# A maximum over the last axis: four blocks with their own partition pitch in place of one pitch of 512 KB

## The chip, the cores and the metric

The kernel runs on one core of a Trainium2 chip. The metric is the device time of one execution in microseconds (us); lower is better. Medians of several runs are quoted. The "span" of a profile (164.7 us for the kernel before) is about 1.8 us shorter than the device time of that same execution (166.5 us).

## The reference

```python
x = np.random.randn(32, 512, 1024).astype(np.float32)
def reference(x):
    return np.max(x, axis=-1).astype(np.float32)
```

These are 16,384 rows of 1,024 floats (4 KB each, 67.1 MB in all), and one maximum per row. Spread over 128 partitions, each partition has 128 rows.

## The kernel before

One queue (SyncE's) loads groups of rows into a ring buffer of 46 rows per partition. VectorE takes the maximum of each group as soon as it has landed. The number of rows of each group is in `ROWS`; the groups become smaller so that little work is left when the last one lands.

```python
ROWS = [10, 13, 12, 10, 9, 8, 7, 7, 6, 5, 5, 4, 4, 3, 3, 3, 3, 2, 2, 2, 2, 2, 1, 1, 1, 1, 1]
RING = 46
...
xr = xf.rearrange("(p i) d -> p i d", p=P)      # partition p holds rows 128p .. 128p+127
...
for g in ROWS:
    if at + g > RING:
        at = 0
    xc = ring[:, at:at + g, :]
    nc.sync.dma_start(out=xc, in_=xr[:, b:b + g, :])
    nc.vector.reduce_max(out=res[:, b:b + g], in_=xc, axis=X)
    at += g
    b += g
    if not stored and b >= I - 16:
        stored = b
        nc.scalar.dma_start(out=out_r[:, :b], in_=res[:, :b])
# the last row in two halves
for h in range(2):
    xh = ring[:, at, h * H:(h + 1) * H]
    nc.sync.dma_start(out=xh, in_=xr[:, b, h * H:(h + 1) * H])
    nc.vector.reduce_max(out=part[:, h:h + 1], in_=xh, axis=X)
nc.vector.tensor_tensor(...max of the two halves...)
nc.scalar.dma_start(out=out_r[:, stored:], in_=res[:, stored:])
```

A load of g rows reads 4g KB in one piece for each partition. One such piece is a packet in the profile, and a load has landed when all 128 of its packets are in. The pieces of neighbouring partitions start 128 x 4 KB = 512 KB apart in memory. This distance is the pitch.

Of the kernel before, what the change touches and what calls it, by code (L numbers as in the profile page):

```python
# [1 line left out]

# [4 lines left out]


F32 = mybir.dt.float32


ROWS = [10, 13, 12, 10, 9, 8, 7, 7, 6, 5, 5, 4, 4, 3, 3, 3, 3, 2, 2, 2, 2, 2, 1, 1, 1, 1, 1]
RING = 46


@with_exitstack
def kernel(
    ctx: ExitStack,
    tc: tile.TileContext,
    x: bass.AP,  # L20
    out: bass.AP,
):
    nc = tc.nc
    P = 128
    X = mybir.AxisListType.X

    xf = x.flatten_outer_dims()
    N, D = xf.shape
    H = D // 2
    I = N // P  # L30

    xr = xf.rearrange("(p i) d -> p i d", p=P)
    of = out.flatten_outer_dims()
    out_r = bass.AP(tensor=of.tensor, offset=of.offset, ap=[[I, P], [1, I]])

    once = ctx.enter_context(tc.tile_pool(name="once", bufs=1))
    ring = once.tile([P, RING, D], F32)
    res = once.tile([P, I], F32)
    part = once.tile([P, 2], F32)

    b = at = 0
    stored = 0
    for g in ROWS:
        if at + g > RING:
            at = 0
        xc = ring[:, at:at + g, :]
        nc.sync.dma_start(out=xc, in_=xr[:, b:b + g, :])
        nc.vector.reduce_max(out=res[:, b:b + g], in_=xc, axis=X)  # L48
        at += g
        b += g  # L50
        if not stored and b >= I - 16:
            stored = b
            nc.scalar.dma_start(out=out_r[:, :b], in_=res[:, :b])

    assert b == I - 1 and at + 1 <= RING
    for h in range(2):
        xh = ring[:, at, h * H:(h + 1) * H]
        nc.sync.dma_start(out=xh, in_=xr[:, b, h * H:(h + 1) * H])
        nc.vector.reduce_max(out=part[:, h:h + 1], in_=xh, axis=X)  # L59
    nc.vector.tensor_tensor(  # L60
        out=res[:, b:b + 1], in0=part[:, 0:1], in1=part[:, 1:2],
        op=mybir.AluOpType.max,
    )
    nc.scalar.dma_start(out=out_r[:, stored:], in_=res[:, stored:])


# [1 line left out]
_INS = ['x']  # L68
_OUTS = [((32, 512), 'float32')]


# [23 lines left out]
```

## Time and profile before

| quantity | value | read from |
|---|---|---|
| device time, median | 166.26 us | three runs (166.19 to 166.53) |
| span | 164.7 us | the page |
| VectorE busy | 139.5 us | the page, part 1 |
| DMA engines busy from 16 us to 144 us | 0.98 to 1.01 | the windows view |
| VectorE's first wait | 15.8 us | the timeline |

These lines are from the page of the kernel before: part 1 (busy time of an engine), and the share of the chain that ended last (the waits and the work, followed back from the last instruction to what released each).

```profile
...
DVE 139.5 (85%) x30; POOL 0.2 (0%) x4
...
DMA 70%; DVE 28%; issue 0%
DMA ring<-in_x_dram 70%; DVE res L48 27%; DVE part L59 1%; DVE res L60 0%
...
```

The next lines are the windows view of the kernel before. The columns are the stretch, its length, VectorE's busy time, POOL's, the clock, the busy share of the DMA engines, and GB/s.

```profile
...
core 0: us, DVE busy (x) POOL busy (x), PEclk, DMA share, GB/s
0.00:16.00 16.00, 0.18 (x1) 0.20 (x4) 1.00 0.92 381
16.00:32.00 16.00, 11.09 (x2) 0.00 (x0) 1.00 0.98 422
32.00:48.00 16.00, 15.50 (x2) 0.00 (x0) 1.00 1.00 434
48.00:64.00 16.00, 16.00 (x2) 0.00 (x0) 1.00 1.01 439
64.00:80.00 16.00, 15.97 (x3) 0.00 (x0) 1.00 0.99 427
...
```

The DMA engines are full at 422 to 439 GB/s in the stretches from 16 us on that are shown, while VectorE has a little room. The last lines are VectorE's timeline: start, length, instruction, how many were merged, and in brackets the idle time before the first of them with what ended it.

```profile
...
15.82 10.82 DVE L48 TENSOR_REDUCE res<-ring 128x10 f32<-128x10240 f32 x1 [15.82 <-DMA ring<-in_x_dram]
31.56 14.02 DVE L48 TENSOR_REDUCE res<-ring 128x13 f32<-128x13312 f32 x1 [4.91 <-DMA ring<-in_x_dram]
46.08 49.61 DVE L48 TENSOR_REDUCE res<-ring 128x12 f32<-128x12288 f32 x5 [0.50 <-DMA ring<-in_x_dram]
96.50 43.73 DVE L48 TENSOR_REDUCE res<-ring 128x7 f32<-128x7168 f32 x9 [0.81 <-DMA ring<-in_x_dram]
140.55 9.93 DVE L48 TENSOR_REDUCE res<-ring 128x3 f32<-128x3072 f32 x4 [0.33 <-DMA ring<-in_x_dram]
150.77 10.25 DVE L48 TENSOR_REDUCE res<-ring 128x2 f32<-128x2048 f32 x7 [0.29 <-DMA ring<-in_x_dram]
...
```

VectorE waits 15.82 us for the first 10 rows and 4.91 us for the next 13. After that it waits only for fractions of a microsecond, but it does so four more times: it follows the landings closely until the end.

### The profile page before, as it was taken

What the parts mean: (1) busy time and instruction counts of PE and PEld (TensorE: products, weight loads), DVE (VectorE), ACT (ScalarE), POOL (GpSimd) and SP (SyncE); (2) the same over time, 40 slices, a digit from 0 to 9 for tenths busy, and PEclk for the clock granted to TensorE, in tenths of its full rate; (3) what the DMA queues carried; (4) which work ended last, traced back from release to release, by engine and by line L of the source; (5) the groups of instructions that cost most, each with busy time, mean ns of one, the idle gap of its engine ahead of it and who ended that gap; (6) DMA issues with size and microseconds to landing.
All of it is one profiled execution on the core that took longest, in us unless ns stands there. A gap on an engine that the chain in (4) does not pass through costs nothing.

```text
span 164.7 us, 118 instructions
## 1 busy us (share of the span) xinstructions
DVE 139.5 (85%) x30; POOL 0.2 (0%) x4
## 2 busy tenths in 40 slices
DVE  0001994399989999999999989999999999999994
POOL 0000000000000000000000000000000000000000
DMA  6998999999989999999999999999999999999960
GB/s 199 438 467 376 453 465 453 436 406 394 469 388 467 444 430 430 408 438 425 439 432 425 426 431 419 428 438 409 438 430 421 427 421 421 420 418 421 408 260 2
DMA packets 4464, 67.18 MB, mean 408 GB/s; under 512 B 752, under 2 KB 752, under 8 KB 1648
## 3 DMA queue, kind: packets, MB, share of 16 engines
q1 hardware_dynamic: 4176, 67.11, 95.8%
q10 hardware_dynamic: 288, 0.07, 0.2%
HBM read 67.11 MB, written 0.07 MB: 408 GB/s over the span
## 4 chain that ended last, share of the span: by engine, by line
DMA 70%; DVE 28%; issue 0%
DMA ring<-in_x_dram 70%; DVE res L48 27%; DVE part L59 1%; DVE res L60 0%
## 5 line engine op out<-in xcount | busy, mean ns | idle before, releaser
L48 DVE TENSOR_REDUCE res<-ring 128x2 f32<-128x2048 f32 (+11 forms) x27 | 138.1, 5165 | 22.9 <-DMA ring<-in_x_dram 22.7
L59 DVE TENSOR_REDUCE part<-ring 128x1 f32<-128x512 f32 x2 | 1.3, 676 | 0.0
L60 DVE TENSOR_TENSOR res<-part 128x1 f32<-128x1 f32 x1 | 0.2, 159 | 0.0
L79 POOL MEMSET const-bfloat16-1.0<- 128x1 bf16 x1 | 0.1, 101 | 0.0
L79 POOL MEMSET const-uint8-127<- 128x1 uint8 x1 | 0.1, 101 | 0.0
L79 POOL MEMSET const-float32-0.0<- 128x1 f32 x1 | 0.1, 98 | 0.2 <-issue 0.2
L79 POOL MEMSET const-float32-1.0<- 128x1 f32 x1 | 0.1, 98 | 0.0
## 6 DMA issues: line engine op xcount, KB each, us to landing
ring<-in_x_dram SPq DMA_DIRECT2D x2, 5120.0 KB, 35.6
ring<-in_x_dram SPq DMA_DIRECT2D x2, 3584.0 KB, 33.0
ring<-in_x_dram SPq DMA_DIRECT2D x1, 6656.0 KB, 30.4
ring<-in_x_dram SPq DMA_DIRECT2D x1, 6144.0 KB, 44.4
ring<-in_x_dram SPq DMA_DIRECT2D x4, 1536.0 KB, 38.9
ring<-in_x_dram SPq DMA_DIRECT2D x2, 2560.0 KB, 38.1
ring<-in_x_dram SPq DMA_DIRECT2D x5, 1024.0 KB, 22.2
ring<-in_x_dram SPq DMA_DIRECT2D x1, 4608.0 KB, 43.1
```

Source lines behind the costliest of these rows:

```text
L48: nc.vector.reduce_max(out=res[:, b:b + g], in_=xc, axis=X)
L59: nc.vector.reduce_max(out=part[:, h:h + 1], in_=xh, axis=X)
L60: nc.vector.tensor_tensor(out=res[:, b:b + 1], in0=part[:, 0:1], in1=part[:, 1:2], op=mybir.AluOpType.max,)
L79: nc = _bacc.Bacc("TRN2", target_bir_lowering=False, num_devices=1)
```

## The change

It cuts the 128 rows per partition into four blocks of 42, 35, 34 and 17 rows. Each block is a contiguous part of the input and of the output, laid over the 128 partitions by itself, so its pitch is 168, 140, 136 or 68 KB. Each block has its own store. A loop over the blocks replaces the old one, so the sizes of the loads change as well (the first is of 15 rows in place of 10), and the last row is no longer halved. The intent, as far as the diff tells it, is to get away from a large power of two as the pitch.

```diff
-ROWS = [10, 13, 12, 10, 9, 8, 7, 7, 6, 5, 5, 4, 4, 3, 3, 3, 3, 2, 2, 2, 2, 2, 1, 1, 1, 1, 1]
+BLOCKS = [
+    [15, 14, 13],
+    [11, 9, 8, 7],
+    [6, 6, 5, 4, 4, 4, 3, 2],
+    [2, 2, 2, 2, 2, 1, 1, 1, 1, 1, 1, 1],
+]
 ...
-    xr = xf.rearrange("(p i) d -> p i d", p=P)
 ... (the old loop, its two stores and the halved last row go)
+    at = first = 0
+    for loads in BLOCKS:
+        S = sum(loads)
+        xb = xf[first * P:(first + S) * P, :].rearrange("(p i) d -> p i d", p=P)
+        b = 0
+        for g in loads:
+            if at + g > RING:
+                at = 0
+            xc = ring[:, at:at + g, :]
+            nc.sync.dma_start(out=xc, in_=xb[:, b:b + g, :])
+            nc.vector.reduce_max(out=res[:, first + b:first + b + g], in_=xc, axis=X)
+            at += g
+            b += g
+        dst = bass.AP(tensor=of.tensor, offset=of.offset + first * P, ap=[[S, P], [1, S]])
+        nc.scalar.dma_start(out=dst, in_=res[:, first:first + S])
+        first += S
```

The change is thus three changes in one: the pitch, the sizes of the loads (with the tail), and the number of stores.

More of the change, by code (lines that the diff above doesn't have):

```diff
@@ L28 @@
     N, D = xf.shape
-    H = D // 2
     I = N // P
-    xr = xf.rearrange("(p i) d -> p i d", p=P)
     of = out.flatten_outer_dims()
-    out_r = bass.AP(tensor=of.tensor, offset=of.offset, ap=[[I, P], [1, I]])
     once = ctx.enter_context(tc.tile_pool(name="once", bufs=1))
@@ L38 @@
     res = once.tile([P, I], F32)
-    part = once.tile([P, 2], F32)
-    b = at = 0
-    stored = 0
-    for g in ROWS:
-        if at + g > RING:
-            at = 0
-        xc = ring[:, at:at + g, :]
-        nc.sync.dma_start(out=xc, in_=xr[:, b:b + g, :])
-        nc.vector.reduce_max(out=res[:, b:b + g], in_=xc, axis=X)
-        at += g
-        b += g
-        if not stored and b >= I - 16:
-            stored = b
-            nc.scalar.dma_start(out=out_r[:, :b], in_=res[:, :b])
-    assert b == I - 1 and at + 1 <= RING
-    for h in range(2):
-        xh = ring[:, at, h * H:(h + 1) * H]
-        nc.sync.dma_start(out=xh, in_=xr[:, b, h * H:(h + 1) * H])
-        nc.vector.reduce_max(out=part[:, h:h + 1], in_=xh, axis=X)
-    nc.vector.tensor_tensor(
-        out=res[:, b:b + 1], in0=part[:, 0:1], in1=part[:, 1:2],
-        op=mybir.AluOpType.max,
-    )
-    nc.scalar.dma_start(out=out_r[:, stored:], in_=res[:, stored:])
+    at = first = 0
[14 more added lines that the diff above has]
+        first += S
+    assert first == I
 _INS = ['x']
```

## The prediction

> **What bounds the kernel now.** The windows view shows the DMA engines 0.98 to 1.01 busy in every 16 us stretch from 16 us to 144 us, at 422 to 439 GB/s; VectorE is busy 139.5 us of 164.7 (the page). So the load stream sets the time, and VectorE (the maximum) follows closely. The chain of waits is 70% DMA and 28% VectorE.
>
> Taking the trace's packets one by one: a load of g rows makes one packet of 4g KB per partition. Medians are 161 ns (4 KB), 311 (8 KB), 1514 (40 KB), 1966 (52 KB): 10 ns plus 150.3 ns per 4 KB, that is 27.3 GB/s an engine, 436 GB/s for sixteen. This is the fabric ceiling of the Trainium skill ("DMA: Bandwidth & Descriptors", section "Where 436 GB/s comes from": 435.2 GB/s), and the trace agrees. The same page's section "Latency and other measured facts" lists a 512 KiB pitch at 207 GB/s a direction against 214 for a padded pitch. This trace doesn't show such a loss: with the pitch at 512 KB, all time above the packet floor is 1.4 us an engine of 157.6, and 0.7 us of it is the very first packet of each engine, where I take it for start-up, not pitch.
>
> **What the change does.** Pitch: 168, 140, 136 and 68 KB in place of 512 KB. I expect it to buy almost nothing, at most the few tenths of excess. Loads: 27 in place of 29, which saves about 0.16 us of packet overhead an engine. Stores: four of 128 short packets in place of two; from the 448 B (25 ns) and 64 B (10 ns) packets I estimate 0.2 us more of each engine. The last row's two halves and the combining maximum (0.68 + 0.68 + 0.16 us) become one reduction of 1.21 us.
>
> The row schedule matters more. A reduction of g rows occupies VectorE about 0.065 + 1.067 g us, a load lands 0.08 + 1.20 g us after the one before. Before, VectorE waits 15.8 us for 10 rows and 4.9 us for the next 13; later waits total 1.9 us. With 15, 14, 13 rows first, I work out landings at about 21.8, 38.7 and 54.4 us, with waits of about 0.8 and 0.6 us; then VectorE never waits again. From 54.4 us on 99 rows in 25 reductions take 107.3 us, so VectorE ends at about 161.8 us, against 162.4. Loads end at about 160 (160.7 before). The ring doesn't starve: each slot comes free over 10 us before the stream needs it. The first three stores are off the chain; the last goes out from the last reduction, as before (1.4 us to land).
>
> **Prediction.** The span falls from 164.7 to about 164.1 us, the time from 166.26 to about 165.7 us; range 164.9 to 166.6. Chances: faster by over 2% 0.03, within 2% 0.95, slower by over 2% 0.02.
>
> **What would show it.** Right: packet medians unchanged; DMA share still about 1.0; VectorE idle about 21.8, 0.8 and 0.6 us and none after 54 us; VectorE busy about 139.5 us; chain: DMA for a third, then VectorE for two thirds. Wrong about the pitch: first-packet excess gone (saves up to 0.7 us), or packets above the floor in some block (loads land later, VectorE waits after 54 us).
>
> **What could make it wrong.** A stall of one engine (before has one of 0.8 us near 66 us; after 54 us mine would be hidden by VectorE's backlog, earlier not). [...] A load held back by a semaphore shared with a store: before, one load waited 5.0 us for the first store, harmless because of the queue's depth.

## The result, and the profile after

The changed kernel takes 165.47 us (median of four runs, 165.37 to 165.61), the kernel before 166.22 us in the same rounds (166.0 to 166.53). The ratio is 0.9954, with a 95% interval from 0.9936 to 0.9972: faster by about half a per cent. The time lies in the predicted range, 0.2 us below the predicted value.

The page of the changed kernel, the same lines as before:

```profile
...
DVE 138.4 (85%) x27; POOL 0.2 (0%) x4
...
DVE 74%; DMA 23%; DVEq 1%; another core or an unknown queue 0%; SPq 0%; issue 0%
DVE res L52 74%; DMA ring<-in_x_dram 23%; DVEq L84 1%; SPq L51 0%
...
```

DVEq and SPq are the instruction sequencers of VectorE and SyncE. The chain has turned over: DMA 70% and VectorE 28% before, VectorE 74% and DMA 23% now. VectorE's timeline of the changed kernel shows why:

```profile
...
21.39 16.15 DVE L52 TENSOR_REDUCE res<-ring 128x15 f32<-128x15360 f32 x1 [21.39 <-DMA ring<-in_x_dram]
38.33 15.09 DVE L52 TENSOR_REDUCE res<-ring 128x14 f32<-128x14336 f32 x1 [0.79 <-DMA ring<-in_x_dram]
54.06 107.19 DVE L52 TENSOR_REDUCE res<-ring 128x13 f32<-128x13312 f32 x25 [0.64 <-DMA ring<-in_x_dram]
```

There are three waits (21.39, 0.79 and 0.64 us), and from 54.06 us on 25 reductions run without a pause for 107.19 us. The windows view of the changed kernel, same columns as before:

```profile
...
0.00:16.00 16.00, 0.00 (x0) 0.20 (x4) 1.00 0.90 369
16.00:32.00 16.00, 10.61 (x1) 0.00 (x0) 1.00 1.08 467
32.00:48.00 16.00, 15.21 (x2) 0.00 (x0) 1.00 1.00 434
48.00:64.00 16.00, 15.36 (x2) 0.00 (x0) 1.00 0.98 422
64.00:80.00 16.00, 16.00 (x3) 0.00 (x0) 1.00 0.96 411
...
```

The stretches scatter more than before (467 GB/s in one, 411 in another), as packets of up to 60 KB count where they start; the four from 16 us to 80 us average 433 GB/s, against 430 before. The stream is as full as it was.

To see whether the pitch changes the rate, I took the packets of both traces one by one. This is not a view of the profile but a summary of its packet records; each is one partition's piece of one load:

```
packet      median ns, 512 KB pitch    median ns, changed kernel
 4 KB               161                       161.5
 8 KB               311                       311
36 KB              1364                      1364
52 KB              1966                      1966
```

In these traces the steady rate doesn't depend on the pitch. It is 10 ns plus 150.3 ns per 4 KB (below I call this time of a packet its floor); the slope alone is 436 GB/s for sixteen engines.

So where do the 0.75 us come from? In the profiled executions VectorE ended at 162.40 us before and at 161.25 us after. But one thing in the first trace looked accidental: near 66 us two packets took 0.36 and 0.79 us more than the others of their size, and from there on every landing was 0.69 us later than the sum of the packets explains. If that was an accident, the baseline of my arithmetic was wrong, and so was the credit that it gave to the sizes of the loads.

### The profile page after: what moved, and what is told of

The parts are those of the page before. It is cut to its first block, busy times and chain, and to the rows that moved or that the text cites. A ratio compares the mean times of both kernels' runs of the same rounds, so it can differ in the third digit from the quotient of the medians.

```text
span 163.6 us, 114 instructions
## 1 busy us (share of the span) xinstructions
DVE 138.4 (85%) x27; POOL 0.2 (0%) x4
## 4 chain that ended last, share of the span: by engine, by line
DVE 74%; DMA 23%; DVEq 1%; another core or an unknown queue 0%; SPq 0%; issue 0%
DVE res L52 74%; DMA ring<-in_x_dram 23%; DVEq L84 1%; SPq L51 0%
## 5 line engine op out<-in xcount | busy, mean ns | idle before, releaser
L52 DVE TENSOR_REDUCE res<-ring 128x1 f32<-128x1024 f32 (+12 forms) x27 | 138.4, 5205 | 22.8 <-DMA ring<-in_x_dram 22.8
```

The lines of the kernel that those rows point to most:

```text
L52: nc.vector.reduce_max(out=res[:, first + b:first + b + g], in_=xc, axis=X)
```

## The experiments

There were two theories. "Schedule" is the one of the prediction: the sizes of the loads bring the gain, the pitch nothing. "Pitch" is the rival: the pitch brings it, and the slow packets in the first trace are its work. In the edits below, `BLOCKS` lists the rows of each block (128 means one pitch of 512 KB), `ROWS` the loads, `STORES` the row counts after which a store is issued; the loop is the one of the changed kernel with these three lists kept apart.

### a_again: the kernel before, unchanged

> The kernel before, unchanged, against itself: ratio 1.000, and a second trace of it. Its first trace shows two disturbances that the changed kernel's trace lacks: two packets near 66 us that took 0.36 and 0.79 us too long, after which all landings are 0.69 us later, and a first landing about 0.4 us later than the packet floor explains. Without them I work out that its VectorE would end at 161.1 to 161.4 us in place of 162.40, no later than the changed kernel's 161.25. If they are accidents of that one execution (theory 'schedule'), they will not be at the same place here. If they come from the pitch (rival 'pitch'), this trace shows such slow packets again, an excess of several tenths of a us.

It took 166.02 us, ratio 0.9998 (0.9986 to 1.0011). No slow packet appears near 66 us, nor any other above 16 ns over the floor after 8 us. Yet VectorE ended at 161.95 us, 0.45 us before its end in the first trace but later than the 161.1 to 161.4 us that I had worked out. The disturbance near 66 us was thus not repeated; it was worth about 0.4 us in that one execution. The late first landing was no accident, as VectorE's timeline shows:

```profile
...
15.98 10.82 DVE L48 TENSOR_REDUCE res<-ring 128x10 f32<-128x10240 f32 x1 [15.98 <-DMA ring<-in_x_dram]
31.69 14.02 DVE L48 TENSOR_REDUCE res<-ring 128x13 f32<-128x13312 f32 x1 [4.90 <-DMA ring<-in_x_dram]
...
```

The first landing is as late as in the first trace, or later (15.98 against 15.82 us), with no disturbed packet to blame after the start.

### b_new_rows_one_pitch: only the pitch undone

```diff
-BLOCKS = [42, 35, 34, 17]
+BLOCKS = [128]
 ROWS = [15, 14, 13, 11, 9, 8, 7, 6, 6, 5, 4, 4, 4, 3, 2, 2, 2, 2, 2, 2, 1, 1, 1, 1, 1, 1, 1]
 STORES = [42, 77, 111, 128]
```

> Only the pitch undone: the loads and the four stores of the changed kernel, from one pitch of 512 KB. Theory 'schedule': the time of the changed kernel, 165.4 to 165.6 us, ratio 0.995 to 0.997; VectorE waits 21.4 to 21.8, 0.8, 0.6 us and then never. Rival 'pitch': 165.8 to 166.4 us, ratio 0.998 or more, with slow packets in the first 54 us that delay VectorE.

It took 165.89 us, ratio 0.9994 (0.9981 to 1.0006). The new sizes alone bring at most 0.3 us by the interval, and 0.1 us by the value. VectorE's timeline:

```profile
...
21.95 16.15 DVE L63 TENSOR_REDUCE res<-ring 128x15 f32<-128x15360 f32 x1 [21.95 <-DMA ring<-in_x_dram]
38.87 15.09 DVE L63 TENSOR_REDUCE res<-ring 128x14 f32<-128x14336 f32 x1 [0.76 <-DMA ring<-in_x_dram]
54.60 107.19 DVE L63 TENSOR_REDUCE res<-ring 128x13 f32<-128x13312 f32 x25 [0.65 <-DMA ring<-in_x_dram]
```

Set this beside the changed kernel's lines. The second and third waits are the same to 0.03 us, and the long run of 25 reductions has the same 107.19 us. The only difference is the first wait, 21.95 in place of 21.39 us, and everything after it is 0.54 to 0.56 us later. This speaks against "schedule", and also against my picture of "pitch": there is no slow packet later on; the whole loss lies before the first landing.

### c_new_rows_one_pitch_two_stores: fewer stores

```diff
 BLOCKS = [128]
-STORES = [42, 77, 111, 128]
+STORES = [113, 128]
```

> The changed kernel's loads, one pitch of 512 KB, two stores (113 and 15 rows). If the number of stores costs nothing on the chain of waits, the same as with four stores within 0.1 us. If the two extra stores cost, faster by up to 0.2 us.

It took 166.03 us, ratio 1.0004 (0.9991 to 1.0016). Two stores in place of four save nothing; the 0.14 us between the medians are in the wrong direction, and the intervals overlap. Its trace has an accident of its own: many packets between 8 and 115 us are 30 to 280 ns over the floor. VectorE still ran without a pause after its third wait, as its backlog covers such delays.

### d_old_rows_four_pitches: only the pitch changed

```diff
-BLOCKS = [128]
+BLOCKS = [35, 34, 45, 14]
 ROWS = [10, 13, 12, 10, 9, 8, 7, 7, 6, 5, 5, 4, 4, 3, 3, 3, 3, 2, 2, 2, 2, 2, 1, 1, 1, 1, 1]   # + last row in halves
-STORES = [112, 128]
+STORES = [35, 69, 114, 128]
```

> Only the pitch changed: the loads of the kernel before, last row in halves, from four blocks of 35, 34, 45 and 14 rows with their own pitches and four stores. Theory 'schedule': the time of the kernel before, ratio 0.999 to 1.001. Rival 'pitch': VectorE ends at 161.1 to 161.4 us as worked out without disturbances, so the time falls by 0.6 to 1.0 us, ratio 0.994 to 0.997, and the trace has no slow packets after the first of each engine.

It took 165.59 us, ratio 0.9975 (0.9962 to 0.9989): the pitch brings about 0.4 us (d also has four stores in place of two, but by c their number brings nothing), less than the 0.6 to 1.0 us that I had written for the rival. VectorE's timeline:

```profile
...
15.64 10.82 DVE L64 TENSOR_REDUCE res<-ring 128x10 f32<-128x10240 f32 x1 [15.64 <-DMA ring<-in_x_dram]
31.36 14.02 DVE L64 TENSOR_REDUCE res<-ring 128x13 f32<-128x13312 f32 x1 [4.90 <-DMA ring<-in_x_dram]
45.89 49.46 DVE L64 TENSOR_REDUCE res<-ring 128x12 f32<-128x12288 f32 x5 [0.51 <-DMA ring<-in_x_dram]
...
```

Against the second trace of the kernel before, the first landing is 0.34 us earlier (15.64 against 15.98 us), and the second is 0.33 us earlier (31.36 against 31.69). After the first landing the two streams are alike: the last load lands 144.34 us after the first in d and 144.33 us after it in a_again. The same holds for the changed kernel (138.20 us) and b (138.16 us). So the pitch costs nothing measurable after the first landing in these four traces.

Both theories had fallen in the form in which I stated them. The new one, "start": the pitch costs some tenths of a microsecond once, while the sixteen DMA engines begin, and the rest follows from the later first landing. The packet records support it. The records don't name the engine, but as no packet of a first load is through in less than 1.5 us, the first sixteen to start are one for each engine:

```
kernel (first load)                        mean start of an engine's first packet
512 KB pitch: before, a_again, b, c            2.14, 2.18, 2.12, 2.15 us
140 or 168 KB: d, after                        1.91, 1.93 us

                                           slowest engine: start plus excess of its first packet
512 KB pitch: before, a_again, b, c            3.37, 3.51, 3.45, 3.30 us
140 or 168 KB: d, after                        3.18, 2.91 us
```

With either pitch the first engine starts at 1.73 to 1.75 us. With 512 KB the others start later on average. But this is only 0.2 us, and the latest of the sixteen starts hardly differs (2.77 us before, 2.76 us in d). The first landing follows the slowest engine, by the sum of its start and of the time by which its first packet exceeds the median of its size (the second part of the table): from before to d this sum falls by 0.19 us and the landing by 0.18 us, from a_again to d by 0.33 and 0.34 us, from b to the changed kernel by 0.55 and 0.56 us. So what the records show is a start of the stream in which the slowest engine loses less; neither the start nor the excess alone accounts for it.

### after_again: the changed kernel once more

> The changed kernel once more, beside the same runs of the kernel before as the others of this call. From the first runs (ratio 0.9954, interval 0.9936 to 0.9972, with one disturbed run of before among four) and the parts (pitch alone 0.9975, rows alone 0.9994) I expect 0.996 to 0.997, 165.4 to 165.6 us.

It took 165.55 us, as expected and within 0.1 us of the first measurement. The ratio came out at 0.9937 (0.9912 to 0.9962), lower than expected, because on this second chip the kernel before was slower and more scattered than on the others (I call it disturbed): its eleven runs lay between 166.10 and 167.38 us. Ratios to the kernel before in this call are therefore not the quiet ones.

### e_first_load_other_pitch: the pitch of one load

This one gives a wrong result: the first load reads other rows than it should, so ten of the 128 columns of results are wrong.

```diff
-        nc.sync.dma_start(out=xc, in_=xr[:, b:b + g, :])
+        if b == 0:
+            src = xf[0:42 * P, :].rearrange("(p i) d -> p i d", p=P)[:, 0:g, :]   # 168 KB pitch
+        else:
+            src = xr[:, b:b + g, :]                                               # 512 KB pitch
+        nc.sync.dma_start(out=xc, in_=src)
```

> The kernel before, of which only the first load (10 rows) takes its rows from a block with a pitch of 168 KB; all other loads keep 512 KB; the result is wrong on purpose in ten columns. Theory 'start': the pitch costs only while the 16 engines begin, so this one load brings the whole gain: first landing at 15.4 to 15.6 us in place of 15.8 to 15.95, all later landings as much earlier, ratio 0.997 to 0.998. Rival 'throughout': the pitch costs a little in every load, so the time stays near that of before, ratio 0.999 to 1.000.

It took 165.69 us, ratio 0.9955 (0.9927 to 0.9983), and its timeline is shown together with the next one.

### f_rest_other_pitch: the converse

Also wrong in ten columns: the loads of experiment d, but the first one from the 512 KB pitch.

> The converse: the old rows from four blocks, but the first load from the 512 KB pitch; wrong on purpose in ten columns. Theory 'start': first landing 15.8 to 15.95 us, ratio 0.999 to 1.001, the gain of four pitches is gone. Rival 'throughout': ratio 0.997 to 0.998 stays.

It took 165.79 us, ratio 0.9949 (0.9927 to 0.9972). VectorE's timeline of e, where only the first load has another pitch:

```profile
...
15.42 10.82 DVE L53 TENSOR_REDUCE res<-ring 128x10 f32<-128x10240 f32 x1 [15.42 <-DMA ring<-in_x_dram]
31.13 14.02 DVE L53 TENSOR_REDUCE res<-ring 128x13 f32<-128x13312 f32 x1 [4.90 <-DMA ring<-in_x_dram]
45.68 49.46 DVE L53 TENSOR_REDUCE res<-ring 128x12 f32<-128x12288 f32 x5 [0.52 <-DMA ring<-in_x_dram]
...
```

And of f, where only the first load keeps the 512 KB pitch:

```profile
...
15.87 10.82 DVE L69 TENSOR_REDUCE res<-ring 128x10 f32<-128x10240 f32 x1 [15.87 <-DMA ring<-in_x_dram]
31.59 14.02 DVE L69 TENSOR_REDUCE res<-ring 128x13 f32<-128x13312 f32 x1 [4.91 <-DMA ring<-in_x_dram]
46.13 49.46 DVE L69 TENSOR_REDUCE res<-ring 128x12 f32<-128x12288 f32 x5 [0.51 <-DMA ring<-in_x_dram]
...
```

The traces answer the question as "start" has it. Changing one load moves the first landing to 15.42 us and with it the second and third by the same 0.45 us, measured against f on the same chip; f, which puts only that load back, lands at 15.87 us like the kernel before. The mean start of an engine's first packet is 1.88 us in e and 2.11 us in f, the slowest engine's start plus excess 2.96 and 3.41 us. Each side of this rests on one trace.

The times do not settle it. "Start" expected a ratio of 0.999 to 1.001 for f, and it missed: f got 0.9949. e missed its 0.997 to 0.998 too. The likely cause is the disturbed kernel before, for f's time of 165.79 us is below the quiet runs of the kernel before by only 0.1 to 0.2 us (165.92 and 166.00). But e and f themselves, side by side, differ by only 0.10 us in their medians, where "start" wants about 0.45 us; even without e's two slowest runs (166.17 and 166.59 us) it is about 0.15 us. The two profiled executions took 165.47 and 165.81 us. That the first load alone brings the whole gain is thus shown by the traces, not by the times. And there is a pattern in the spread: on this chip f and the changed kernel, whose loads after the first are not from 512 KB, stayed within 0.28 us (165.66 to 165.94 and 165.44 to 165.72); e and the kernel before, whose later loads are, spread over 1.12 and 1.28 us (165.47 to 166.59 and 166.10 to 167.38). e's own trace has four packets 0.30 to 0.49 us over the floor near 34 us.

### g_even_rows: other sizes of loads, with the new pitches

The reductions need 1.07 us a row, the loads 1.20 us. For VectorE to be done one reduction after the last landing, no load may be larger than what the rest of the stream gives VectorE as a lead. Working back from the last row gives these sizes:

```diff
-BLOCKS = [42, 35, 34, 17]
-ROWS = [15, 14, 13, 11, 9, 8, 7, 6, 6, 5, 4, 4, 4, 3, 2, 2, 2, 2, 2, 2, 1, 1, 1, 1, 1, 1, 1]
-STORES = [42, 77, 111, 128]
+BLOCKS = [45, 34, 35, 14]
+ROWS = [7, 14, 13, 11, 10, 9, 8, 7, 6, 5, 5, 4, 4, 3, 3, 3, 2, 2, 2, 2, 1, 1, 1, 1, 1, 1, 1, 1]
+STORES = [45, 79, 114, 128]
```

> Both gains together: blocks of 45, 34, 35 and 14 rows with their own pitches, and loads of 7, 14, 13, 11, 10, 9, 8, 7, 6, 5, 5, 4, 4, 3, 3, 3, four of 2 and eight of 1 row, sized so that no reduction starts so late that the rest of VectorE's work ends after the last load. From landings 0.08 + 1.20 g apart and reductions of 0.142 + 1.067 g us I work out that VectorE ends 0.3 to 0.55 us before that of the changed kernel: 165.0 to 165.2 us, ratio 0.994 to 0.995. If the rows make no difference: as the changed kernel.

It took 164.86 us (164.74 to 164.98), ratio 0.9894 (0.9872 to 0.9916) against the disturbed kernel before, the best of all. The result is correct. I had expected 165.0 to 165.2 us, so it came out below the range. Its timeline:

```profile
...
11.64 7.62 DVE L63 TENSOR_REDUCE res<-ring 128x7 f32<-128x7168 f32 x1 [11.64 <-DMA ring<-in_x_dram]
28.58 15.09 DVE L63 TENSOR_REDUCE res<-ring 128x14 f32<-128x14336 f32 x1 [9.32 <-DMA ring<-in_x_dram]
44.32 116.46 DVE L63 TENSOR_REDUCE res<-ring 128x13 f32<-128x13312 f32 x26 [0.65 <-DMA ring<-in_x_dram]
```

VectorE ends at 160.78 us, and the last load lands at 159.53 us. That is about one reduction of one row (1.22 us) later, so with these loads and this order of work VectorE's side has hardly anything left to give.

### a_third, b_second, d_second, h_even_rows_one_pitch: again on a third chip, and g's rows from one pitch

> The kernel before a third time. On the first chip of these experiments its runs lay within 165.8 and 166.1 us, on the second between 166.1 and 167.4 us, where kernels with several pitches stayed within 0.3 us. Theory 'start' alone: runs within 0.3 us of each other, packets slow only at the start. Theory 'start and disturbance' (a pitch of 512 KB is also more open to slow packets later on, at times and not on every chip): if this chip is like the second, a spread above 0.5 us again, and the trace shows an excess above the packet floor after 8 us of some tenths of a us at one place or another; if it is like the first, nothing of it.

> The rows of the changed kernel from one pitch of 512 KB, again. On a quiet chip 0.999 to 1.000 as before. Where the kernel before is disturbed, this one should be less so, as VectorE's backlog hides what happens after 54 us: ratio 0.995 to 0.998 and a spread below that of the kernel before. First landing 21.8 to 22.0 us either way.

> The old rows from four pitches, again: 165.5 to 165.8 us with a spread within 0.3 us on either kind of chip. First landing 15.4 to 15.65 us. Ratio 0.997 to 0.998 on a quiet chip, lower on one that disturbs the kernel before.

```diff
-BLOCKS = [45, 34, 35, 14]
+BLOCKS = [128]
 ROWS = [7, 14, 13, 11, 10, 9, ...]      # as in g
```

> The rows of 7, 14, 13, 11 and so on from one pitch of 512 KB: parts the gain of that version (164.86 us) in two. Theory 'start': first landing 0.3 to 0.5 us later than 11.62 us and all else as much later, 165.2 to 165.4 us on a quiet chip. If the pitch did nothing there: 164.8 to 165.0 us.

This chip was quiet: the kernel before took 165.92 us (165.78 to 166.17). The kernel before against itself (a_third) gave 165.98 us and 1.0001, b_second 165.87 us and 0.9993 (0.9980 to 1.0007), d_second 165.66 us and 0.9980 (0.9967 to 0.9993), h 165.35 us and 0.9965 (0.9952 to 0.9977). So the parts came out as on the first chip. (d_second's first landing, 15.70 us, is just outside the 15.4 to 15.65 us that I had expected.) a_third's trace does show packets of 30 to 240 ns over the floor, mostly between 46 and 62 us, yet no larger spread, and its last load landed 144.43 us after its first, against 144.33 us in a_again: these packets cost at most 0.1 us. The disturbance of the second chip didn't come back, so its cause stays open.

h beside g separates that version's gain. VectorE's timeline of h:

```profile
...
12.13 7.62 DVE L63 TENSOR_REDUCE res<-ring 128x7 f32<-128x7168 f32 x1 [12.13 <-DMA ring<-in_x_dram]
29.06 15.09 DVE L63 TENSOR_REDUCE res<-ring 128x14 f32<-128x14336 f32 x1 [9.31 <-DMA ring<-in_x_dram]
44.80 116.43 DVE L63 TENSOR_REDUCE res<-ring 128x13 f32<-128x13312 f32 x26 [0.65 <-DMA ring<-in_x_dram]
```

The first landing is 0.49 us later than g's (12.13 against 11.64 us), all else is as much later, and so is the time: 165.35 against 164.86 us, which are from different chips. The first wait with each pitch, over all traces:

| first load | 512 KB pitch | 140 to 180 KB pitch |
|---|---|---|
| 7 rows | 12.13 | 11.64 |
| 10 rows | 15.82, 15.98, 15.86, 15.87 | 15.64, 15.70, 15.42 |
| 15 rows | 21.95, 21.89, 21.98 | 21.39, 21.54 |

No value of one column reaches into the other. By the means the difference is 0.3 us for 10 rows and about 0.5 us for 7 and 15 rows. The slowest engine's start plus excess divides in the same way: 3.28 to 3.51 us in the eight traces with 512 KB, 2.74 to 3.24 us in the six others.

## Why the prediction was right, and where its reasons failed

- The time was right, 165.7 us predicted and 165.47 us measured, and the range held it. In part this was luck. A gain of 0.6 us was credited to the sizes of the loads and next to nothing to the pitch; measured by themselves, the sizes brought about 0.1 us and the pitch 0.3 to 0.4 us, so two errors nearly cancelled. The range of 164.9 to 166.6 us would have held an unchanged time of 166.26 us as well. What the prediction really worked out is experiment b: VectorE was to end at 161.8 us, and it ended at 161.79 us in b, with the pitch of 512 KB, but at 161.25 us in the changed kernel. VectorE's picture was right: waits of 21.8, 0.8 and 0.6 us were predicted, 21.39, 0.79 and 0.64 us measured; no wait after 54 us; 107.3 us predicted for the last 25 reductions and 107.19 us measured; a chain of mostly VectorE (74%; I had written two thirds). Its busy time was not: 138.4 us in place of the 139.5 us expected. The page's 27 reductions of 5205 ns on average sum to 140.5 us, 2.1 us more than the busy time, as each of the 24 that start right behind another overlaps it by about 0.09 us; in the kernel before only 19 start like that.
- "I expect it to buy almost nothing, at most the few tenths of excess", of the pitch: the throughput part was right, the packet medians are unchanged. But the few tenths were the larger part of the gain. The pitch alone gave 0.9975 and 0.9980, about 0.3 to 0.4 us, with the old sizes of loads.
- "0.7 us of it is the very first packet of each engine, where I take it for start-up, not pitch": this step failed. It is start-up, but its cost to the first landing depends on the pitch. I looked only at how long the first packets took, and that excess did not go away (0.65 us an engine before, 0.74 us after). What changed is the slowest engine's start and excess together, 3.37 us before and 2.91 us after; the engines' first packets began at 2.14 us on average before and at 1.93 us after.
- "The row schedule matters more": this failed. The new sizes alone gave 0.9994 and 0.9993, about 0.1 us. They trade later waits for a longer first one: at the same pitch VectorE's waits for DMA sum to 22.4 us in a_again and to 23.4 us in b, and what b wins back is about as much busy time (139.3 us in a_again, 138.4 us in b). That sizes can matter is shown by g and h: h, from one pitch, is 0.57 us faster than the kernel before.
- "against 162.4": this number was the error behind it. It came from one execution with a stall, which I had seen and named, but still used as the baseline. Without it VectorE ended at 161.95 us in the second trace of the kernel before. A gain of 0.6 us was claimed for the sizes; most of that was the stall of the execution they were compared with.
- "from the 448 B and 64 B packets I estimate 0.2 us more of each engine", for the stores: no cost of the number of stores showed; c, with two, took 0.14 us longer than b, with four.
- The measured 0.75 us between the medians is more than the parts add up to. The product of the quiet ratios, 0.9975 x 0.9994 = 0.997, is 0.5 us. The remaining 0.25 us fit the baseline, which was not repeated on that chip: the kernel before had a median of 166.22 us in that comparison, against 166.00 and 165.92 us on the two quiet chips, and the four executions behind the 166.22 us include one at 166.53 us. That this is the reason is not shown.

What stays open: why the slowest engine loses more at the start with a pitch of 512 KB (no record here shows what it waits for), whether it is the power of two or only the size of the pitch (no pitch above 180 KB other than 512 KB was run; a smaller pitch also means that the first load's pieces lie in a shorter stretch of memory), and what disturbed the kernels with later loads at 512 KB on the second chip. There is a hint only: after 8 us, packets more than 0.2 us over the floor appear in four of the eight traces whose later loads have the 512 KB pitch (before, a_third, c, e) and in none of the six others, where the largest excess is 0.19 us.

## What to carry to other kernels

A baseline trace is one execution: before a plan counts tenths of a microsecond against it, look for single packets far above their size's median and subtract them, or take a second trace. In these traces a later first landing made all later landings as much later (0.54 to 0.56 us in b against the changed kernel), so in a stream that keeps the DMA engines full, look at the layout of the very first load by itself; here, on quiet chips, it was where the pitch counted. In g the sizes of a shrinking series of loads were found by working back from the end, so that VectorE was done one small piece after the last landing; the same can be tried where a consumer follows a stream.

## What the Trainium skill lacked or had wrong

- "DMA: Bandwidth & Descriptors", section "Latency and other measured facts", row on the row pitch at large powers of two: for loads from memory into the on-chip buffer it gives nothing. Here a 512 KB pitch cost no throughput (36 KB packets 1364 ns with either pitch, and 144.33 or 144.34 us from first to last landing). It cost 0.3 to 0.5 us once, at the first landing.
- The same page, section "Where 436 GB/s comes from": its ceiling of 435.2 GB/s agrees with the packets' slope of 150.3 ns per 4 KB, which is 436 GB/s for sixteen engines. The section also says that for transfers between memory and the on-chip buffer a limit of about 358 GB/s binds, half of what two cores share; with this core alone in use by the program it did not (408 GB/s over the span of the kernel before).
- The same page has, beside a latency to the first byte, nothing on the first packet of each engine in a stream: here it took up to 1.3 us longer than the later ones of its size, and the sixteen engines began between 1.72 and 3.29 us.
- "VectorE: DVE Perf Modes", section "The perf-mode tier table", gives `tensor_reduce` as 1x only, and for another operation at 1x 2293 ns for 2048 float32 elements, which is 1.12 ns an element with its fixed part: the trace agrees, as 14020 ns for 13 rows against 1208 ns for one in the kernel before is 1.04 ns an element without the fixed part.
- No page that I read has the spread that one chip of three showed: the kernel before between 166.10 and 167.38 us in eleven runs, beside 165.44 to 165.72 us of the changed kernel in six.
